# New durations in the engine model that orders a TensorE-bound two-layer kernel

## Chip, cores and metric

One core of one Trainium2 chip. The metric is the device time of one execution in microseconds (us).

## The reference, cut to what matters

One step of a streaming encoder with two layers, for a prompt of 2048 tokens and for 8 samples of 16 new tokens each. The width is 1024, with 8 heads of 128. All arrays are float32.

```python
def trunk(x, c, pos, ...):                       # for the prompt, and again for the samples
    for i in range(2):
        shift, scale, gate = split(silu(c) @ w_ada[i] + b_ada[i])
        h = rmsnorm(x, norm_pre[i]) * (1 + scale) + shift
        if i == 0:    # gated DeltaNet, chunked: conv of q, k, v; then per head
            qkv, z, a, b = split(h @ w_in_gdn)
            q, k, v = silu(causal_conv(qkv)), q and k normalized
            # (I + A)^-1, A strictly lower triangular, applied to v and k; then a scan over the chunks:
            #   u = u_i - w_i @ s;   o = qg_i @ s + qk_i @ u;   s = s * g_i + kd_i^T @ u
            out = (rmsnorm(o) * silu(z)) @ w_out_gdn
        else:         # differential attention, block-causal
            q, k, v, z = split(h @ w_in_diff); q, k = rope(q), rope(k)
            a = softmax(q1 @ k1^T / 8) - lam * softmax(q2 @ k2^T / 8)
            out = (rmsnorm(a @ v) * silu(z)) @ w_out_diff
        x = x + gate * rmsnorm(out, norm_post[i])
```

It returns both outputs and all states, convolution rows, keys and values.

## The kernel before

**Tiles and stages.** The 17 tiles of 128 rows (16 of the prompt, one of the samples) are worked in two halves, of 9 and 8 tiles. Each half passes through four stages: DeltaNet heads (`gdn_heads`), output projection (`out_proj`), attention heads (`diff_heads`), output projection. In the profile these are 100 to 840, 840 to 1000, 1000 to 1640 and 1640 to 1800 us for the first half, and 1800 to 2430, 2430 to 2590, 2590 to 3410 and from 3410 for the second; before 100 us stand the adaptation vectors and the first normalization. Tiles go through the projections in groups of up to three.

**Projections.** `mm3s` (944) makes a float32-like product out of three fp32r matmuls for each 128 rows of the contraction: operands are split into a rounded part and the rest. Weights pass through a staging tile `st` and are split on ACT, VectorE (DVE) and GpSimd (POOL) by `load` (535) into `wq` and `wz`.

**DeltaNet, a head.** `conv` (1182) ends in a Tanh, `gate_out` (1174) is a Silu for z, `decay` (1281) an Exp. `keys` (1242) works out row factors by small GpSimd instructions and powers (tile `sm`). `inverse` (1384) inverts I + A: the 16x16 blocks on VectorE in `blocks` (1335; tiles `Lx`, `Lw`, `Lt`, `Lr`), then merged by small matmuls that use the array as 32x32, 64x32 and 64x64 tiles (`X`, `V`, `W`, `Y`, `F`, `Wf`). `scan` (1504) carries the state: a matmul, `y` on VectorE, a matmul, the copy `r` on ACT, a matmul, the new state `S` on VectorE.

**Attention, a head.** `rotate` applies the rotary embedding (tile `r`), `scores` and `expo` make score pieces of up to 512 keys: VectorE takes the negated maximum `negm`, ACT the exponential `p` with its sum. `weigh` works out the factors `fj`, GpSimd scales the first map's piece, `join` adds the second map's on VectorE, `flip` transposes on TensorE and copies to `at` on ACT or VectorE, `values` multiplies with `vpc`, and `finish` normalizes with a power on GpSimd (`fo`).

**What sets the order.** The order of instructions on TensorE, VectorE, ACT and GpSimd is fixed when the kernel is built, by the class `Weave`. Each of the functions above is a generator, a stream. It yields the engine that it needs next, an event or a tile to wait for. `run` (281) goes in steps: for each stream that can go on it takes the time at which its next instruction could start, the later of the stream's own time and `free_at` of the engine, and lets the earliest one emit its instructions; of equal ones that with the higher priority. Projections have a low priority, so they fill TensorE where nothing else is ready. After every instruction `account` (130) adds its price, `c`, in ns, to the engine's time and notes when its output is ready; `HOP` adds a constant for a result that passes from one engine to another. `either` (206), `copy` (211), `modulate` (699) and `flip` also ask `free_at` which of two engines would be free earlier. The engines then run their instructions in that order on the chip, each waiting for semaphores where an operand is late.

**A duplicate.** A second copy of `queries` (1797) to `scan_sample` of the DeltaNet stage, and of `conv_outputs`, `diff_loads` and the start of `diff_heads`, stands inside a first `diff_heads` (1662). The complete definition of `diff_heads` at line 2149 takes the place of that one before anything is called.

All instructions are emitted through line 105, so the profile gives them that line, and they are told apart by tiles.

Of the kernel before, what the change touches and what calls it, by code (L numbers as in the profile page):

```python
# [12 lines left out]
F32 = mybir.dt.float32  # L13
# [74 lines left out]
class Weave:  # L88
# [23 lines left out]
    def __init__(self, tc, kept):  # L112
        nc = tc.nc
        self.tc = tc
        self.kept = kept
        self.ordered = True
        self.queue_at = self.dma_at = 0.0
        self.parts = {}
        self.free_at = dict(pe=0.0, v=0.0, s=0.0, g=0.0, sy=0.0)
        self.ready = {}  # L120
        self.ev = {}
        self.places = {}
        self.held = {}
        self.streams = []
        self.cur = None
        self.n = 0
        for key, real in (("pe", nc.tensor), ("v", nc.vector), ("s", nc.scalar), ("g", nc.gpsimd), ("sy", nc.sync)):
            setattr(self, key, Weave._Engine(self, key, real))

    def account(self, key, op, args, kw):  # L130
# [4 lines left out]
        n = 1  # L135
# [4 lines left out]
        if key == "pe":  # L140
            if op == "transpose":
                c = (2 if rest[0].dtype == F32 else 1) * max(n, out.shape[0]) * 0.417 + 2
            elif rest[0].dtype == F32:
                c = 4 * max(n, rest[0].shape[-1]) * 0.417 / (4 if out.shape[0] <= 32 else 1)
            else:
                c = max(n, 2 * rest[0].shape[-1]) * 0.417 + 2
        elif key == "v":
            fast = op in ("tensor_copy", "tensor_scalar", "memset") and all(a.space != PSUM for a in rest)
            c = 75 + n * (0.52 if fast else 1.04)
            if op in ("scalar_tensor_tensor", "tensor_scalar") and any(a.shape[-1] == 1 for a in rest):  # L150
                c += 60
            if op == "memset":
                c = 60 + 0.26 * n
        elif key == "s":
# [3 lines left out]
            elif rest[0].space != PSUM:  # L158
                c += 32
        elif key == "g":  # L160
# [12 lines left out]
        start = self.free_at[key]  # L173
# [157 lines left out]
def body(ctx, tc, I, O):  # L331
# [1330 lines left out]
    def diff_heads(hi_, tiles_of, pool, ahead):  # L1662
# [134 lines left out]
        def queries(h, gi, d):  # L1797
            nt = len(tiles_of[gi])
            yield ("conv", h, gi, 0),
            yield ("sq", h, gi),  # L1800
            sq, sm = d["sq"], d["sm"]
            pt = yield from turn(d["q"], nt * P)
            yield from squares(pt, nt * P, sq[:, 1])
            W.free(pt)
            yield "g"
            g.tensor_scalar(sm[:, 3, 0:nt], sq[:, 1, 0:nt], 128.0 * EPS, 512.0 * EPS * EPS, op0=ALU.mult, op1=ALU.add)
            yield ("xq", h, gi),
            W.free(sq)
            for i in range(nt):
                yield from product(d, i, d["q"], d["E"])  # L1810
            W.done(("qk", h, gi))

        def product(d, i, src, out):
            c = slice(i * P, (i + 1) * P)
            ps = yield from bank()
            pe.matmul(ps[:, 0:P], d["k"][:, c], src[:, c], start=True, stop=True)
            yield "v"
            v.scalar_tensor_tensor(out=out[:, i, :], in0=ps[:, 0:P], scalar=d["sm"][:, 2, i:i + 1],
                                   in1=d["E"][:, i, :], op0=ALU.mult, op1=ALU.mult)
            W.free(ps)  # L1820

        def blocks(area, nl):

            X, Wl = (pool.tile([24, 16, 16], F32, name=k, bufs=1) for k in ("Lx", "Lw"))
            wf = Wl.rearrange("p i j -> p (i j)")

            yield "sy"
            sy.dma_start(X[0:nl], bass.AP(area[0].tensor, area[0].offset, [[16 * P + 16, nl], [P, 16], [1, 16]]))
            g.memset(wf[0:nl], 0.0)
            g.memset(wf[0:nl, ::17], 1.0)  # L1830
            yield "v"
            T, R = (pool.tile([24, k], F32, name=nm, bufs=1) for k, nm in ((512, "Lt"), (64, "Lr")))

            def at(a, o, *dims):
                return bass.AP(a.tensor, a.offset + o, [a[0:nl].ap[0], *([st, k] for st, k in dims)])

            def four(a, r, c, nr, ncol):

                return at(a, r * 16 + c, (4 * 17, 4), (16, nr), (1, ncol))

            v.tensor_copy(four(Wl, 0, 3, 3, 1), four(X, 0, 3, 3, 1))
            for j in (2, 1):
                sh = [nl, 4, j, 4 - j]
                t = at(R, 0, (j * (4 - j), 4), (4 - j, j), (1, 4 - j))
                v.tensor_tensor(out=t, in0=four(X, 0, j, j, 1).broadcast_to(sh),
                                in1=four(Wl, j, j, 1, 4 - j).broadcast_to(sh), op=ALU.mult)
                o = four(Wl, 0, j, j, 4 - j)
                v.tensor_tensor(out=o, in0=o, in1=t, op=ALU.add)
            for m in (4, 8):
                def corner(a, s_, r, c):  # L1850
                    return at(a, s_ * 2 * m * 17 + r * m * 16 + c * m, (16, m), (1, m))

                def product(A, B, out):
                    for i in range(8 // m):
                        v.tensor_tensor(out=at(T, i * m ** 3, (m * m, m), (m, m), (1, m)),
                                        in0=A[i][:, :, None, :].broadcast_to([nl, m, m, m]),
                                        in1=B[i].rearrange("p k c -> p c k")[:, None].broadcast_to([nl, m, m, m]),
                                        op=ALU.mult)
                    for i in range(8 // m):
                        v.tensor_reduce(out=out[i], in_=at(T, i * m ** 3, (m * m, m), (m, m), (1, m)), axis=AX.X,  # L1860
                                        op=ALU.add)

                Rs = [at(R, i * m * m, (m, m), (1, m)) for i in range(8 // m)]
                X12, W11, W12, W22 = ([corner(a, i, *rc) for i in range(8 // m)]
                                      for a, rc in ((X, (0, 1)), (Wl, (0, 0)), (Wl, (0, 1)), (Wl, (1, 1))))
                product(X12, W22, Rs)
                product(W11, Rs, W12)
            yield "sy"
            sy.dma_start(bass.AP(area[1].tensor, area[1].offset, [[256, nl], [1, 256]]), wf[0:nl])

        def inverse(h, gi, d):

            nt = len(tiles_of[gi])
            h0, h1 = slice(0, 64), slice(64, P)
            X = yield from new([P, 3, P], "X", NX, "v")
            yield ("E", h, gi),
            for i in range(nt):
                yield from product(d, i, d["k"], X)
            W.done(("xq", h, gi))
            area = yield from W.hold(areas, "area", "sy")  # L1880
            sy.dma_start(area[0][0:nt, 0:P * P].rearrange("t (p c) -> p t c", c=P), X[:, 0:nt])
            yield from blocks(area, 8 * nt)
            W16 = yield from new([P, 3, 16], "W16", 2, "sy")
            sy.dma_start(W16[:, 0:nt], area[1][0:nt].rearrange("t (p c) -> p t c", c=16))
            W.free(area)
            Wt = yield from new([P, 3, 32], "W", 2, "v")
            v.tensor_tensor(out=Wt[:, 0:nt].rearrange("p t (a c) -> p t a c", c=16),
                            in0=W16[:, 0:nt, None, :].broadcast_to([P, nt, 2, 16]),
                            in1=C("same").rearrange("p (a c) -> p a c", c=16)[:, None].broadcast_to([P, nt, 2, 16]),
                            op=ALU.mult)  # L1890
            W.free(W16)
            V = yield from new([P, 3, 32], "V", 2, "v")
            Y = yield from new([P, 3, 32], "Y", 2, "s")
            F = yield from new([P, 3, 64], "F", 2, "s")
            pi = yield from bank("v")

            def area_of(o, n):
                return pi[:, o:o + nt * n].rearrange("p (t c) -> p t c", c=n)

            pa, pb, pf, pt = area_of(0, 32), area_of(96, 32), area_of(192, 64), area_of(0, 64)  # L1900
            quarters = [slice(32 * b, 32 * b + 32) for b in range(4)]

            def each(out, a, b):

                for o, x, y in zip(out, a, b):
                    pe.matmul(o, x, y, start=True, stop=True)

            def parts(t, rows, cols=slice(0, 32)):
                cols = cols if isinstance(cols, list) else [cols] * len(rows)
                return [t[r, i, c] for r, c in zip(rows, cols) for i in range(nt)]  # L1910


            yield "v"
            v.transpose(V.rearrange("p t c -> p (t c)")[:, 0:32 * nt], Wt.rearrange("p t c -> p (t c)")[:, 0:32 * nt])
# [778 lines left out]
```

## Time and profile before

| | us |
|---|---|
| median of 3 runs | 3558.8 |
| lowest, highest | 3554.32, 3575.8 |
| the profiled execution | 3559.35 |
| its span, first to last instruction | 3557.6 |
| mean granted TensorE clock in it | 0.977 |

PE is TensorE's matmuls and PEld its weight loads, DVE is VectorE, POOL is GpSimd. A name such as `ps<-S,q` says which tile is written and which are read, by the program's names. [...]

### The profile page before, as it was taken

To read this page: it belongs to the slowest core of one execution; us is meant where nothing else is said; L and a number is where in the kernel's file an instruction comes from. 1 tells how busy PE (TensorE), PEld (TensorE's weight loads), DVE (VectorE), ACT (ScalarE), POOL (GpSimd) and SP (SyncE) were. 2 spreads that over 40 slices of the span, in tenths; PEclk is the share of its full clock that TensorE was granted. 3 is DMA by queue.
4 is the path that set the end of the run, shared out by engine and by line. 5 is a ranking of instruction groups with operands and counts; after the bars stand their busy time and mean duration, and the time that the engine had idled before them with its cause. 6 is when DMAs were issued, how large, how long until landed. Compare 5 with 4: busy or idle time off the path is not lost.

```text
span 3557.6 us, 79075 instructions
## 1 busy us (share of the span) xinstructions
PE 3390.2 (95%) x28952; PEld 3151.5 (89%) x28952; DVE 2531.9 (71%) x6462; ACT 1763.0 (50%) x5376; POOL 1560.0 (44%) x2836
## 2 busy tenths in 40 slices
PE   5999999999999999999999999998899999999988
PEld 2887789889999999998989899888898999999988
DVE  4677788776576666666567777775588878888872
ACT  3454455553354444444445555553365555555541
POOL 4344444443444344333434554544444444444432
PEclk6999999999999999999999999998999999999999
DMA  5225432236343333444432222224311112111113
GB/s 191 59 64 169 122 77 69 61 98 195 124 130 112 112 114 114 122 120 136 159 91 50 58 62 74 60 75 161 125 42 49 37 55 57 52 52 41 47 57 125
DMA packets 479420, 330.59 MB, mean 93 GB/s; under 512 B 65799, under 2 KB 442143, under 8 KB 479030
## 3 DMA queue, kind: packets, MB, share of 16 engines
q1 hardware_dynamic: 474358, 316.76, 30.0%
q0 software_dynamic: 4672, 8.78, 1.0%
q8 instruction: 227, 3.72, 0.4%
q14 instruction: 163, 1.34, 0.1%
HBM read 233.65 MB, written 91.77 MB: 91 GB/s over the span
## 4 chain that ended last, share of the span: by engine, by line
PE 37%; DVE 7%; POOL 3%; ACT 2%; issue 2%; DMA 1%; SPq 0%; POOLq 0%; DVEq 0%; ACTq 0%
PE ps L105 37%; DVE p L105 1%; DVE negm L105 1%; DVE Lt L105 1%; POOL sm L105 1%; POOL p L105 1%; POOL fo L105 1%; ACT jkg L105 0%; DVE wq L105 0%; DVE rz L105 0%; DVE Lr L105 0%; DMA st<-in_w_in_diff_dram 0%; ACT L105 0%; DMA ro<-og 0%; ACT at L105 0%
## 5 line engine op out<-in xcount | busy, mean ns | idle before, releaser
L105 PE MATMUL ps<-wq,hT 128*128 128x256 f32 x6120 | 851.4, 287 | 4.2 <-DVE r L105 3.1
L105 PEld LDWEIGHTS ps<-wq,hT 128*128 128x128 f32 x6120 | 775.2, 191 | 16.9 <-DVE r L105 3.5
L105 PE MATMUL ps<-hT,wq 128*128 128x384 f32 (+1 forms) x3456 | 696.4, 341 | 2.7 <-ACT ub L105 2.2
L105 PE MATMUL ps<-wz,hT 128*128 128x256 f32 x4488 | 647.4, 292 | 13.3 <-DVE r L105 12.1
L105 PEld LDWEIGHTS ps<-wz,hT 128*128 128x128 f32 x4488 | 581.9, 194 | 23.6 <-DVE r L105 12.8
L105 PEld LDWEIGHTS ps<-hT,wq 128*128 128x128 f32 x3456 | 557.2, 190 | 15.8 <-ACT ub L105 3.1
L105 ACT ACTIVATE p<-ps,negm 128x512 f32<-128x512 f32 (+3 forms) x640 | 397.1, 624 | 225.5 <-DVE negm L105 220.3
L105 DVE TENSOR_REDUCE negm<-ps 128x1 f32<-128x512 f32 (+3 forms) x640 | 375.0, 606 | 66.6 <-PE ps L105 55.5
L105 PE MATMUL ps<-kst,qst 128*128 128x512 f32 (+3 forms) x1280 | 346.7, 379 | 2.8 <-ACT p L105 2.7
L105 POOL TENSOR_SCALAR p<-p,fj 128x512 f32<-128x512 f32 (+2 forms) x320 | 230.8, 732 | 231.4 <-DVE fj L105 165.5
L105 PE MATMUL ps<-vpc,at 128*128 128x128 f32 x2176 | 294.9, 278 | 7.9 <-ACT at L105 6.2
L105 PEld LDWEIGHTS ps<-vpc,at 128*128 128x128 f32 x2176 | 274.5, 193 | 20.7 <-ACT at L105 10.8
L105 DVE SCALAR_TENSOR_TENSOR p<-p,fj,p 128x512 f32<-128x512 f32 (+2 forms) x320 | 248.4, 803 | 23.3 <-POOL p L105 22.8
L105 ACT COPY at<-ps 128x512 f32<-128x512 f32 (+3 forms) x258 | 132.7, 515 | 234.2 <-PE ps L105 228.9
L105 PEld LDWEIGHTS ps<-kst,qst 128*128 128x128 f32 x1280 | 205.8, 190 | 20.2 <-ACT p L105 6.0
L105 POOL TENSOR_TENSOR wq<-st,wq 128x512 fp32r<-128x512 f32 x110 | 150.5, 1370 | 162.0 <-ACT wq L105 92.0
L105 PE MATMUL ps<-cst_ident,p 128*128 128x128 f32 x1224 | 195.3, 277 | 18.9 <-DVE hT L105 7.9
L105 POOL TENSOR_TENSOR fo<-fo,cpow 128x1 f32<-128x1 f32 x280 | 175.5, 627 | 23.3
L105 ACT ACTIVATE jk<-ps 128x128 f32<-128x128 f32 (+1 forms) x212 | 80.4, 379 | 201.6 <-PE ps L105 145.6
L105 PEld LDWEIGHTS ps<-cst_ident,p 128*128 128x128 f32 x1224 | 144.7, 142 | 27.7 <-DVE hT L105 9.1
L105 POOL TENSOR_SCALAR fo<-so 128x1 f32<-128x1 f32 x144 | 32.3, 224 | 269.0 <-ACT jk L105 255.7
L105 POOL TENSOR_SCALAR fo<-so,sm 128x1 f32<-128x1 f32 x136 | 50.3, 370 | 211.5 <-ACT jkg L105 211.2
(328 smaller groups left out, 6413.2 us busy)
## 6 DMA issues: line engine op xcount, KB each, us to landing
st<-in_w_in_gdn_dram SPq DMA_DIRECT2D x128, 256.0 KB
st<-in_w_in_diff_dram SPq DMA_DIRECT2D x256, 128.0 KB
x<-x SPq DMA_DIRECT2D x34, 512.0 KB
wz<-in_w_ada_dram SPq DMA_DIRECT2D x16, 1024.0 KB
sp<-in_cache_k_dram SPq DMA_DIRECT2D x64, 256.0 KB
sp<-in_cache_v_dram SPq DMA_DIRECT2D x64, 256.0 KB
zg<-zt SPq DMA_DIRECT2D x68, 128.0 KB
og<-o SPq DMA_DIRECT2D x136, 64.0 KB
```

Source lines behind the costliest of these rows:

```text
L105: r = f(*args, **kw)
```

## The change

Prices in `account` get new values, and a change of the array's tiling on TensorE and a change of function table on ACT get a price of their own, `hold`, that is added before the instruction's start. Two fields are added, for the tiling and the table in use. The duplicate described above (498 lines) is taken out. Nothing else is changed.

```diff
@@ Weave.__init__
         self.parts = {}
+        self.tiling = P, P
+        self.table = None
@@ Weave.account
-        n = 1
+        n, hold = 1, 0
...
         if key == "pe":
+            rows, cols = (next(k for k in (32, 64, P) if a <= k) for a in (rest[0].shape[0], rest[0].shape[-1]))
             if op == "transpose":
-                c = (2 if rest[0].dtype == F32 else 1) * max(n, out.shape[0]) * 0.417 + 2
+                c = max(n, out.shape[0]) * (0.85 if rest[0].dtype == F32 else 0.65)
             elif rest[0].dtype == F32:
-                c = 4 * max(n, rest[0].shape[-1]) * 0.417 / (4 if out.shape[0] <= 32 else 1)
+                c = 4 * max(n, rest[0].shape[-1]) * 0.434 / (4 if cols == 32 else 1) / (2 if rows == 32 else 1)
             else:
-                c = max(n, 2 * rest[0].shape[-1]) * 0.417 + 2
+                c = max(n, 192) * 0.434 + 6
+
+            if (rows, cols) != self.tiling:
+                hold = 100 if self.tiling == (P, P) else 120
+                self.tiling = rows, cols
         elif key == "v":
             fast = op in ("tensor_copy", "tensor_scalar", "memset") and all(a.space != PSUM for a in rest)
             c = 75 + n * (0.52 if fast else 1.04)
             if op in ("scalar_tensor_tensor", "tensor_scalar") and any(a.shape[-1] == 1 for a in rest):
                 c += 60
+            if op == "tensor_tensor" and len(out.shape) == 4 and out.shape[-1] <= 8:
+                c = 75 + 2.06 * n
...
         elif key == "s":
             c = 60 + 0.83 * n + (95 if "accum_out" in kw else 0)
             if any(isinstance(kw.get(k), bass.AP) for k in ("bias", "scale")):
                 c += 85
             elif rest[0].space != PSUM:
                 c += 32
+
+            table = {AF.Silu: "silu", AF.Exp: "exp", AF.Ln: "ln", AF.Tanh: "silu exp"}.get(kw.get("func"))
+            if table and self.table not in table.split():
+                hold = 1280
+                self.table = table.split()[-1]
         elif key == "g":
...
             else:
-                c = (240 if len(rest) > 1 else 155) + 0.84 * n
+                c = (240 if len(rest) > 1 or n < 8 else 155) + 0.84 * n
             if op == "tensor_tensor" and kw.get("op") == ALU.pow:
-                c = 300 + 160 * n
+                c = 390 + 170 * n
...
-        start = self.free_at[key]
+        start = self.free_at[key] + hold
@@ inside the first diff_heads
-        def queries(h, gi, d):
...
```

## Rows read from the trace of the kernel before

**Rows 1.** The page: busy us, share and instructions of each engine.
```profile
PE 3390.2 (95%) x28952; PEld 3151.5 (89%) x28952; DVE 2531.9 (71%) x6462; ACT 1763.0 (50%) x5376; POOL 1560.0 (44%) x2836
```
**Rows 2.** Busy time by stage; columns as in the first line.
```profile
core 0: us, PE busy (x) PEld busy (x) DVE busy (x) ACT busy (x) POOL busy (x), PEclk, DMA share, GB/s
0.00:100.00 100.00, 60.14 (x343) 33.19 (x343) 45.84 (x105) 36.08 (x79) 40.20 (x64) 0.71 0.56 179
100.00:840.00 740.00, 716.33 (x6462) 641.54 (x6461) 569.69 (x1592) 381.15 (x1243) 326.17 (x720) 0.99 0.33 93
...
1000.00:1640.00 640.00, 639.26 (x5796) 612.02 (x5795) 439.57 (x1238) 298.83 (x954) 261.90 (x491) 1.00 0.41 117
...
1800.00:2430.00 630.00, 599.46 (x5601) 551.28 (x5600) 477.40 (x1306) 346.81 (x1130) 306.33 (x627) 0.97 0.25 66
...
2590.00:3410.00 820.00, 793.90 (x6076) 748.50 (x6074) 675.91 (x1592) 465.88 (x1383) 377.92 (x582) 1.00 0.18 50
```
**Rows 3.** TensorE's waits, 100 to 840: us in total, times, longest us.
```profile
PE ps L105 <- DVE y L105: 5.1, 3, 2.8
...
PE ps L105 <- ACT r L105: 2.7, 6, 0.6
PE ps L105 <- DVE V L105: 2.5, 5, 0.8
PE ps L105 <- ACT ub L105: 1.9, 1, 1.9
PE ps L105 <- ACT Y L105: 1.6, 2, 1.4
...
PE ps L105 <- ACT zt L105: 1.1, 2, 0.6
```
**Rows 4.** TensorE's waits, 1800 to 2430.
```profile
PE ps L105 <- DVE S L105: 9.5, 4, 5.7
PE ps L105 <- DVE y L105: 6.1, 7, 2.8
PE ps L105 <- DVE V L105: 5.9, 2, 4.5
PE ps L105 <- ACT r L105: 3.7, 8, 0.9
```
**Rows 5.** TensorE's waits, 2590 to 3410.
```profile
PE ps L105 <- ACT at L105: 5.4, 8, 0.8
...
PE ps L105 <- POOL fo L105: 0.8, 1, 0.8
```
**Rows 6.** Busy time, 900 to 950, columns as in rows 2.
```profile
900.00:950.00 50.00, 50.00 (x422) 50.00 (x421) 23.50 (x47) 18.91 (x47) 20.32 (x29) 1.00 0.30 102
```
**Rows 7.** The weight loads' waits, whole span: us in total, times, longest us.
```profile
PEld ps L105 <- issue: 72.8, 222, 4.8
```
**Rows 8.** Instruction groups on VectorE: busy us, mean ns of one, idle before.
```profile
L105 DVE TENSOR_TENSOR Lt<-Lw,Lr 24x512 f32<-24x512 f32 x40 | 48.8, 1220 | 1.4
...
L105 DVE TENSOR_TENSOR Lt<-Lw,Lr 24x64 f32<-24x64 f32 x80 | 21.5, 305 | 0.0
```
**Rows 9.** Timeline of one block inverse: start us, us, instruction, idle before.
```profile
1850.98 2.57 POOL L105 TENSOR_TENSOR wq<-st,wq 128x512 fp32r<-128x512 f32 x2 [0.99 <-ACT wq L105]
...
1851.17 2.50 DVE L105 TENSOR_TENSOR Lt<-Lw,Lr 24x64 f32<-24x64 f32 x2
...
1853.96 1.00 DVE L105 TENSOR_TENSOR Lt<-Lx,Lw 24x512 f32<-24x512 f32 x1
...
1856.79 0.67 DVE L105 TENSOR_REDUCE Lw<-Lt 24x64 f32<-24x512 f32 x1
...
1858.14 0.93 PE L105 MATMUL ps<-V,X 32*32 32x32 f32 x24 [4.49 <-DVE V L105]
```
**Rows 10.** Instruction groups on ACT, columns as in rows 8.
```profile
L105 ACT ACT_TABLE_LOAD x64 | 82.1, 1283 | 8.2 <-DMA c<-in_c_sample_dram 3.7 <-DVE q L105 3.5
```
**Rows 11.** Timeline of ACT around one table load, columns as in rows 9.
```profile
1866.44 0.20 ACT L105 ACTIVATION_READ_ACCUMULATOR jkg<-ps 128x1 f32 x1
1866.66 1.28 ACT L105 ACT_TABLE_LOAD   x1
1867.95 0.42 ACT L105 ACTIVATE E<-E 128x256 f32<-128x256 f32 x1
```
**Rows 12.** Instruction groups on GpSimd, columns as in rows 8.
```profile
L105 POOL TENSOR_TENSOR fo<-fo,cpow 128x1 f32<-128x1 f32 x280 | 175.5, 627 | 23.3
```
**Rows 13.** Busy time around the wait for S, columns as in rows 2.
```profile
2406.00:2412.00 6.00, 0.53 (x2) 0.53 (x3) 5.79 (x17) 0.21 (x1) 0.61 (x2) 0.50 0.42 134
2412.00:2430.00 18.00, 18.00 (x187) 15.78 (x186) 5.68 (x17) 6.27 (x26) 6.88 (x11) 0.80 0.29 87
```
**Rows 14.** The page: the group of the softmax joins, all widths.
```profile
L105 DVE SCALAR_TENSOR_TENSOR p<-p,fj,p 128x512 f32<-128x512 f32 (+2 forms) x320 | 248.4, 803 | 23.3 <-POOL p L105 22.8
```

More of the change, by code (lines that the diff above doesn't have):

```diff
@@ L1795, in rotate @@
             W.done(("k", h, t))
-        def queries(h, gi, d):
[L1798 to L1914, printed above, removed]
-            yield "pe"
-            each(parts(pa, quarters), parts(X, quarters, quarters), parts(V, quarters))
-            yield "s"
-            s.copy(Y[:, 0:nt], pa)
-            yield "pe"
-            each(parts(pb, quarters), parts(Y, quarters), parts(Wt, quarters))
-            yield "v"
-            v.copy_predicated(Wt[:, 0:nt], C("lev").bitcast(U32)[:, None, :].broadcast_to([P, nt, 32]), pb)
-            v.transpose(V.rearrange("p t c -> p (t c)")[:, 0:32 * nt], Wt.rearrange("p t c -> p (t c)")[:, 0:32 * nt])
-            upper, lower = quarters[0::2], quarters[1::2]
-            yield "pe"
-            each(parts(pa, lower), parts(X, upper, lower), parts(V, upper))
-            Wf = d["Wf"] = yield from new([P, 3, P], "Wf", NWF, "g")
-            e = W.either(nt * P)
-            yield e
-            getattr(W, e).tensor_tensor(
-                out=Wf[:, 0:nt].rearrange("p t (a c) -> p t a c", c=32),
-                in0=Wt[:, 0:nt, None, :].broadcast_to([P, nt, 4, 32]),
-                in1=C("quart").rearrange("p (a c) -> p a c", c=32)[:, None].broadcast_to([P, nt, 4, 32]), op=ALU.mult)
-            yield "s"
-            for r in lower:
-                s.copy(Y[r, 0:nt], pa[r])
-            yield "pe"
-            each(parts(pb, upper), parts(Y, lower), parts(Wt, lower))
-            yield "s"
-            for r, c in zip(upper, lower):
-                s.copy(Wf[r, 0:nt, c], pb[r])
-            for i in range(nt):
-                yield "pe"
-                pe.transpose(pf[h0, i], Wf[h0, i, h0], ident[0:64, 0:64])
-            yield "s"
-            s.copy(F[h0, 0:nt], pf[h0])
-            yield "pe"
-            for c in range(64, P, 32):
-                each(parts(pt, [slice(c, c + 32)], slice(0, 64)), parts(X, [h0], slice(c, c + 32)), parts(F, [h0], h0))
-            W.free(X)
-            yield "s"
-            s.copy(F[h1, 0:nt], pt[h1])
-            yield "pe"
-            each(parts(pf, [h0], h0), parts(F, [h1], h0), parts(Wf, [h1], h1))
-            yield "s"
-            s.copy(Wf[h0, 0:nt, h1], pf[h0])
-            W.free(Wt, V, Y, F, pi)
-            W.done(("inv", h, gi))
@@ L1962, in used @@
-        def used(h, gi, i):
-            d = U[h, gi]
-            d["left"] -= 1
-            if d["left"] == 0:
-                W.free(d["k"], d["q"], d["nv"], d["kd"], d["E"], d["Wf"])
-        def scans():
-            for h in range(H):
-                state = None
-                if hi_ > 0:
-                    state = pool.tile([P, P], F32, name="S", bufs=3)
-                    sy.dma_start(state, st_d[h])
-                for gi, tiles in enumerate(tiles_of):
-                    for ev in ("kd", "nv", "qk", "inv"):
-                        yield (ev, h, gi),
-                    d = U[h, gi]
-                    d["norm"] = len(tiles)
-                    for i, t in enumerate(tiles):
-                        if t == S_T:
-                            W.spawn(scan_sample(h, gi, i, d), 4)
-                        else:
-                            ns = pool.tile([P, P], F32, name="S", bufs=3)
-                            yield from scan(h, gi, i, d, state, ns)
-                            state = ns
-                if last:
-                    sy.dma_start(O["state_gdn_prompt"][0, 0, h], state)
-                else:
-                    sy.dma_start(st_d[h], state)
```

273 lines of the change are left out of this document (removed).

## Prediction

> **What bounds the kernel now.** I read the busy times first: TensorE is busy for 3390.2 of 3557.6 us and VectorE, next, for 71% [rows 1]. The time goes down only where TensorE idles or runs at half clock, so the table by stage comes next [rows 2]. The start (0 to 100 us) idles for 40 us and has a granted clock of 0.71. The first DeltaNet stage (100 to 840) idles for 740.00 - 716.33 = 23.7 us, the second (1800 to 2430) for 30.5 us at a clock of 0.97. The first attention stage (1000 to 1640) idles for 0.7 us, the second (2590 to 3410) for 26.1 us. Third, what TensorE waited for in those stages, because each wait tells which result the order of instructions put too early. In the DeltaNet stages these are mostly VectorE results on the path of the state and of the block inverse (y, V, S: 5.1 + 2.5, then 9.5 + 6.1 + 5.9 us) and ACT results (2.7 + 1.9 + 1.6 + 1.1, then 3.7 us) [rows 3, 4]. In the second attention stage they are short, such as eight of at most 0.8 us for the transposed weights `at`, 5.4 us in all [rows 5].
>
> The change touches no computation. The removed 498 lines are a second copy of functions, inside an earlier `diff_heads` that the later definition of that name replaces; no instruction comes from them: nothing. Everything else is prices inside `account`, and prices act in two ways: which stream `run` lets emit next on an engine, and which engine `either`, `copy`, `modulate` and `flip` choose. So nearly all instructions stay the same in number and kind, and what can change is waiting, plus a little work moved between VectorE, ACT and GpSimd.
>
> **TensorE's prices.** In a stretch of little but 256-column matmuls there are 422 starts in 50.00 us, 118.5 ns each [rows 6]. Old price 256 x 0.417 + 2 = 109 ns, new 256 x 0.434 + 6 = 117 ns. No matmul becomes faster by this. A change of array tiling now costs 100 to 120 ns of model time. In the trace the weight loads sit idle 222 times for "issue" alone, 72.8 us in all, 0.33 us each [rows 7]. `run` ranks streams by when they could start, without this extra, so it doesn't group the small matmuls: I leave these 73 us where they are. If the new order had fewer or more switches, I'd bound that by a quarter of them either way, 18 us.
>
> **The block inverse on VectorE.** `blocks` emits its VectorE instructions in one piece, 40 times for three tiles and 8 times for two. Its largest instruction (24x512) was priced 75 + 1.04 x 512 = 607 ns and takes 1220 on average [rows 8]; new price 75 + 2.06 x 512 = 1130. With its two reductions at 607 both before and after, the m = 8 part goes from 2430 to 3474 ns. In the one block that I follow it takes from 1853.96 to 1857.46, 3.5 us, so that part is now priced right. The same block shows the consequence: the 32x32 matmuls on V idle 4.49 us for it [rows 9]. But it also shows what no price holds: a pair of 24x64 products, 305 ns each on average [rows 8], took 2.50 us while GpSimd ran two weight subtractions (2.57 us). So I count half of the VectorE waits as repaired: y, S and V together are 5.1 + 2.5 + 9.5 + 6.1 + 5.9 = 29.1 us [rows 3, 4], half is 14.5 us. Bounds: 0 (all of it is the stretching) and 29.1; a loss by the new order as such is counted once, with the sum.
> [...]
>
> **ACT's table loads.** There are 64, 1283 ns each, priced 0 before and 1280 now [rows 10]. Between silu and exp they alternate in both DeltaNet stages, and as `run` doesn't rank by this extra either, I expect 50 to 80 of them. What goes is the surprise. ACT's waits by TensorE there sum to 2.7 + 1.9 + 1.6 + 1.1 + 3.7 = 11.0 us [rows 3, 4]; the 6.4 us for `r` are 14 short waits for a copy whose price is unchanged, so about 4.6 us can be loads and the instructions queued behind them, and ACT's delay reaches TensorE through VectorE too. I take 6 us, bounds 0 and 11.
> [...]
>
> **GpSimd's prices.** The power goes from 460 to 560 ns (627 measured, [rows 12]), small instructions by 85 ns. GpSimd is busy 44% [rows 1] and in the longest stage TensorE waits for its powers 0.8 us in all [rows 5]; over four such stages worth 0 to 3 us, I take 0.
>
> **The clock.** [...] Over the second DeltaNet stage 0.97 means 0.03 x 630 = 19 us, over the first 0.01 x 740 = 7 us [rows 2], of which idle time is a part that costs nothing. If half of the waits go, I take a third of these 26 us: 9 us, bounds 0 and 20.
>
> **Sum.** 14.5 + 6 + 9 = 29.5 us, all on the path because TensorE sets the end. Start, attention and the output stages: their order is drawn anew too; I take 0 on balance, bounds 15 us either way. The profiled execution took 3559.35 us, 0.6 above the median of the three runs, so both give the same: 3559.4 - 29.5 = **3530 us**, 0.8% less.
>
> **Rivals.** *The gaps close fully:* all 29.1 + 11.0 us of these waits, 20 us of clock, and a good half (14 us) of the second attention stage's 26.1: 74 us, 3485. For it: prices and trace agree closely for m = 8 and the loads. Against: the stretching, and that most prices (the softmax ones among them) stay as they were. *The gain is hidden:* the waits have moved elsewhere, 0 to 12 us, about 3553. For it: 2.50 us for a pair of 0.6. *Slower, by the lost cushion in the softmax chain:* until now a result priced X was covered by X/109 filler matmuls of 118.5 real ns, 8.7% more time than X; now by X/117, 1.3% more. One softmax piece of 512 keys is priced 607 (maximum) + 665 (exp) + 670 (GpSimd scale) + 667 (join) + 485 (copy) = 3094 ns, unchanged, so its cover shrinks by 7.4%, 0.23 us. There are 320 pieces [rows 14], 74 us if every one lands on TensorE: with the 29.5 gained, 3604. It decides from 128 pieces on (29.5 / 0.23). For it: the second attention stage already has such waits [rows 5]. Against: the first idles 0.7 us in 640, so there is more cover than this cushion, and a late result costs only what is not covered by the rounding to whole groups of three matmuls.
>
> **How the numbers follow.** The forecast (3512 to 3548) 0.47, full closing (below 3512) 0.25, hidden (3548 to 3572) 0.15, slower (above 3572, centred on 3604) 0.13. About 1% (36 us: below 3523, above 3594) is what a measurement of this kernel can tell from no change. A third of the forecast's chance lies below 3523, with the full closing 0.40; above 3594 only the softmax rival, with 0.09 of its 0.13; the rest, 0.51, within. Range 3470 (full closing, with 15 us from start and attention) to 3594.
>
> **What would show it.** Right: the table by stage has 10 to 20 us less idle in the DeltaNet stages, the waits for y, S and V halve, the clock of 1800 to 2430 rises to 0.98 or 0.99, matmul groups keep their counts, and table loads stay between 50 and 80. Wrong: the waits for S and V stay as long with GpSimd products beside them (hidden), or the first attention stage, now idle 0.7 us, idles 20 us or more behind `at`, `p` and `negm` (slower). The forecast falls as a whole if the number of tiling switches or table loads changes by more than a third, or if work moved between VectorE and GpSimd decides.

## The result, and the profile after

The changed kernel takes 3591.94 us (median of 5 runs, 3591.56 to 3597.81) where the kernel before, beside it, took 3565.01 (5 runs, 3554.32 to 3575.8): ratio 1.0083, interval 1.0068 to 1.0098. It is 0.8% slower, and the forecast was 0.8% faster. The profiled executions stand 3590.1 to 3557.6 us by their spans, 32.5 us apart.

The page of the changed kernel has the same 28952 matmuls as [rows 1]. They are busy 22.3 us longer (what matmuls take longer at half clock is part of that, and is split off below), and the rest of the 32.5 us is idle time:

```profile
PE 3412.5 (95%) x28952; PEld 3164.6 (88%) x28952; DVE 2555.1 (71%) x6473; ACT 1761.6 (49%) x5373; POOL 1558.1 (43%) x2820
```

To compare stage by stage, the stretches have to begin and end at the same piece of work. I cut both kernels at the first convolution of a half, the first rotation, the first convolution of the second half, its first rotation, and the end of the last output rows (each stretch is one stage with its output projection). Busy time in these stretches, before:

```profile
core 0: us, PE busy (x) PEld busy (x) DVE busy (x) ACT busy (x) POOL busy (x), PEclk, DMA share, GB/s
94.00:965.00 871.00, 840.75 (x7500) 763.24 (x7498) 637.62 (x1711) 427.34 (x1353) 381.23 (x792) 0.99 0.35 102
965.00:1792.00 827.00, 817.30 (x7229) 784.14 (x7230) 548.09 (x1463) 382.23 (x1162) 341.65 (x613) 0.99 0.42 126
1792.00:2557.00 765.00, 723.28 (x6610) 670.43 (x6608) 545.49 (x1427) 393.98 (x1249) 362.95 (x706) 0.97 0.28 80
2557.00:3551.00 994.00, 954.73 (x7332) 904.36 (x7332) 754.69 (x1759) 524.30 (x1537) 432.83 (x666) 0.99 0.19 57
```

And after:

```profile
95.00:1013.00 918.00, 860.04 (x7498) 773.93 (x7496) 634.27 (x1702) 425.12 (x1356) 383.00 (x790) 0.95 0.33 97
1013.00:1853.00 840.00, 822.58 (x7235) 784.73 (x7236) 560.05 (x1461) 385.38 (x1163) 348.98 (x615) 0.99 0.42 124
1853.00:2602.00 749.00, 721.44 (x6604) 671.08 (x6602) 553.69 (x1443) 394.31 (x1247) 353.54 (x692) 0.98 0.29 82
2602.00:3584.00 982.00, 950.67 (x7332) 902.05 (x7332) 759.78 (x1767) 521.28 (x1533) 434.38 (x665) 1.00 0.20 58
```

The first number behind the stretch is its length. The first DeltaNet stage got 47 us longer, the first attention stage 13; the second DeltaNet stage got 16 us shorter, the second attention stage 12. Length less PE busy is idle time: in the first stage it goes from 30.3 to 58.0 us, and its granted clock from 0.99 to 0.95. The trace's record of the clock has two levels, 1 and 0.5 (18 stretches at 0.5 before, 21 after); a granted clock between them is a mean over the stretch, and half clock is the level 0.5. The record splits the loss further: I count half of the time that TensorE works at half clock as lost. That is my estimate; for the 149 matmuls at the end of this document it gives 0.48 x 25 = 12 us where 24.76 - 14.48 = 10.3 were measured. By that count, with the cuts at the exact instants instead of whole us, the first stage lost 27.8 us to more idle time and 20.6 us to more half clock; the second DeltaNet stage won 13.7 us of idle time and lost 1.2 to the clock; the second attention stage won 8.9 and 4.6. What is left when idle time and half clock are taken off differs by under 5 us in each stage, so next to nothing is dearer work. The second half of the tiles gained 28 us, about as much as was forecast in all, though only 16 of them in a stage where the forecast put its gain; the first half lost 60.

**The waits.** TensorE's waits in the first DeltaNet stage after (101 to 851, a stretch that like that of [rows 3] ends with the last steps of the scan):

```profile
PE ps L105 <- ACT r L105: 13.2, 3, 10.1
PE ps L105 <- DMA wz<-in_w_ada_dram: 12.0, 5, 3.4
PE ps L105 <- DVE y L105: 4.2, 2, 2.9
PE ps L105 <- DVE adaC L105: 3.1, 1, 3.1
...
PE ps L105 <- DVE V L105: 1.5, 2, 0.9
PE ps L105 <- DVE S L105: 1.5, 2, 1.1
```

The same scan steps lie in both stretches, but not the same amount of filling work:

```profile
101.00:851.00 750.00, 705.11 (x6225) 623.56 (x6226) 557.63 (x1572) 367.84 (x1222) 317.77 (x709) 0.95 0.30 85
```

These are 6225 matmuls where [rows 2] has 6462. The scan ended some 11 us later than before, and 237 matmuls, most of them of projections, were left to run behind it; that is where the rest of the 47 us shows.

In the second (1861 to 2467, answering to [rows 4]):

```profile
PE ps L105 <- DVE y L105: 7.6, 10, 3.2
PE ps L105 <- ACT zt L105: 1.4, 1, 1.4
...
PE ps L105 <- ACT r L105: 1.3, 4, 0.4
PE ps L105 <- ACT ub L105: 1.3, 1, 1.3
PE ps L105 <- DVE V L105: 1.1, 4, 0.4
PE ps L105 <- ACT Y L105: 1.1, 2, 0.7
...
PE ps L105 <- DVE S L105: 0.6, 2, 0.4
```

And in the second attention stage (2635 to 3442, answering to [rows 5]), where the waits for `at` shrink, those for `p` grow and new ones for `kst` come in:

```profile
PE ps L105 <- DVE p L105: 6.1, 11, 1.2
PE ps L105 <- DVE kst L105: 4.4, 5, 1.8
...
PE ps L105 <- ACT at L105: 1.1, 3, 0.7
```

The views of [rows 5] and of [rows 3] have, before, for `p` and for the weights of the adaptation vectors (`in_w_ada`):

```profile
PE ps L105 <- DVE p L105: 4.0, 7, 0.8
```

```profile
PE ps L105 <- DMA wz<-in_w_ada_dram: 4.6, 3, 3.9
```

In the second DeltaNet stage y, S and V fall from 21.5 to 9.3 us. The waits for ACT there don't fall: `r` goes from 3.7 to 1.3 us, but `r`, `zt`, `ub` and `Y` together from 4.6 to 5.1. In the first stage y, S and V stay (7.6 to 7.2), and two kinds of wait are new in size: one for `r`, and those for the adaptation vectors (their weights and `adaC`). They make 21 of the 28 us of added idle time.

The longest, 10.1 us for `r`, can be read from ACT's timeline (start, us, instruction, in brackets its idle time and what ended it):

```profile
776.95 0.62 ACT L105 CAST wz<-st 128x512 fp32r<-128x512 f32 x1 [0.25 <-DMA st<-in_w_in_gdn_dram]
780.80 0.62 ACT L105 CAST wq<-st 128x512 fp32r<-128x512 f32 x1 [3.23 <-DMA st<-in_w_out_gdn_dram]
782.72 0.62 ACT L105 CAST wz<-st 128x512 fp32r<-128x512 f32 x1 [1.30 <-DMA st<-in_w_in_gdn_dram]
...
787.56 0.53 ACT L105 ACTIVATE ub<-k 128x384 f32<-128x384 f32 x1 [1.50 <-DVE k L105]
787.99 0.25 ACT L105 COPY r<-ps 128x128 f32<-128x128 f32 x1
```

Ahead of the copy `r`, whose operand TensorE had finished at about 778, the model had put casts of weights whose transfers were still under way: ACT's queue stood for 3.23 + 1.30 us for two transfers and 1.50 for `k`, and the scan's next matmul with it. The change gives transfers no new price. The same place in busy time, with what follows:

```profile
777.80:788.30 10.50, 0.39 (x3) 0.10 (x2) 8.49 (x16) 3.52 (x10) 5.96 (x7) 0.50 0.43 117
788.30:800.00 11.70, 11.01 (x118) 9.73 (x119) 8.28 (x20) 4.76 (x20) 3.68 (x5) 0.68 0.19 57
800.00:810.00 10.00, 10.00 (x97) 8.43 (x96) 4.63 (x14) 7.57 (x21) 5.92 (x16) 1.00 0.21 59
```

At 0.68 over 11.70 us the stretch behind the wait costs, by the same estimate, another 0.32 x 11.70 = 3.7 us.

The groups that the prediction counted on hold: weight loads idle for "issue" 74.9 us, 223 times ([rows 7]: 72.8, 222), the 24x512 product takes 1204 ns on average ([rows 8]: 1220), and there are 56 table loads ([rows 10]: 64):

```profile
L105 ACT ACT_TABLE_LOAD x56 | 71.8, 1283 | 8.2 <-DMA c<-in_c_sample_dram 3.5 <-DVE q L105 3.0 <-DVE k L105 0.6
```

### The profile page after: what moved, and what is told of

Its sections match the earlier page's. It is cut to its first block, busy times and chain, and to the rows that moved or that the text cites. A ratio compares the mean times of both kernels' runs of the same rounds, so it can differ in the third digit from the quotient of the medians.

```text
span 3590.1 us, 79032 instructions
## 1 busy us (share of the span) xinstructions
PE 3412.5 (95%) x28952; PEld 3164.6 (88%) x28952; DVE 2555.1 (71%) x6473; ACT 1761.6 (49%) x5373; POOL 1558.1 (43%) x2820
## 4 chain that ended last, share of the span: by engine, by line
PE 36%; DVE 8%; DMA 2%; POOL 2%; issue 2%; ACT 1%; SPq 0%; POOLq 0%; DVEq 0%; ACTq 0%
PE ps L105 36%; DVE p L105 2%; DVE negm L105 1%; DVE Lt L105 1%; POOL p L105 1%; POOL fo L105 0%; DVE wq L105 0%; ACT p L105 0%; DMA ro<-zg 0%; DMA ro<-og 0%; DVE rz L105 0%; DVE Lw L105 0%; DVE kst L105 0%; DVE r L105 0%; SPq L105 0%
## 5 line engine op out<-in xcount | busy, mean ns | idle before, releaser
L105 PE MATMUL ps<-wz,hT 128*128 128x256 f32 x4488 | 639.2, 290 | 10.9 <-DVE r L105 9.6
L105 PEld LDWEIGHTS ps<-hT,wq 128*128 128x128 f32 x3456 | 564.5, 191 | 15.6 <-issue 2.1
L105 POOL TENSOR_SCALAR p<-p,fj 128x512 f32<-128x512 f32 (+2 forms) x320 | 240.8, 764 | 287.1 <-DVE fj L105 232.4
L105 POOL TENSOR_TENSOR wq<-st,wq 128x512 fp32r<-128x512 f32 x104 | 142.6, 1372 | 148.9 <-ACT wq L105 81.9
L105 POOL TENSOR_SCALAR fo<-so,sm 128x1 f32<-128x1 f32 x136 | 59.3, 436 | 245.7 <-ACT jkg L105 244.0
```

What stands on the lines that cost most here:

```text
L105: r = f(*args, **kw)
```

## The experiments

Times are medians; the ratio is to the kernel before, run beside it. "First half" and "second half" are the parts of the profiled span up to and after the last output row of the first half of the tiles.

| kernel | prices: first half, second half | us | ratio, interval | first half | second half |
|---|---|---|---|---|---|
| before | old, old | 3561.8 to 3566.4 | | 1791 | 1767 |
| VectorE +1 ns | old, old | 3569.62 | 1.0010 (0.9997 to 1.0024) | 1813 | 1753 |
| VectorE -1 ns | old, old | 3584.23 | 1.0045 (1.0031 to 1.0060) | 1818 | 1766 |
| after | new, new | 3591.94 | 1.0083 (1.0068 to 1.0098) | 1853 | 1737 |
| after, ACT +1 ns | new, new | 3586.75 | 1.0057 (1.0040 to 1.0074) | 1839 | 1751 |
| after, ACT -1 ns | new, new | 3567.33 | 1.0005 (0.9992 to 1.0017) | 1815 | 1750 |
| new half, old half | new, old | 3624.41 | 1.0169 (1.0149 to 1.0189) | 1856 | 1764 |
| old half, new half | old, new | **3538.78** | 0.9934 (0.9913 to 0.9954) | 1793 | 1746 |
| old DeltaNet 1, then new | mixed, new | 3547.42 | 0.9951 (0.9936 to 0.9967) | 1806 | 1735 |
| matmul prices alone | part, part | 3610.46 | 1.0132 (1.0115 to 1.0148) | 1839 | 1770 |
| tiling price alone | part, part | 3599.99 | 1.0104 (1.0085 to 1.0123) | 1825 | 1776 |
| table loads alone | part, part | 3579.83 | 1.0039 (1.0016 to 1.0063) | 1819 | 1764 |
| VectorE's price alone | part, part | 3643.35 | 1.0225 (1.0206 to 1.0244) | 1849 | 1801 |

**One group of prices at a time.** Each kernel is the one before with one part of the change as it stands in the diff above. GpSimd's prices alone were not tried.

Matmul prices:

> Only the new TensorE durations (matmuls, transposes) on the kernel before; no price for a change of tiling, all other prices old. Theory A (the loss is made in the first DeltaNet stage, because the adaptation weights are taken up later and the z projections, which fill TensorE, are used up behind them): if it is the matmul durations that delay them, this kernel shows most of the loss, +20 to +35 us, the first out projection starts 30 us or more later than before, and the last adaptation matmul lies after 500 us instead of 442. Theory B (the cushion: matmuls priced truer cover the softmax chain less): +20 us or more, but lost in the two attention stages, with the first DeltaNet stage unchanged within 10 us. Theory C (the order is drawn anew by any change of prices, and where the time lands is chance): anywhere from -25 to +35, with places that change from kernel to kernel.

Tiling:

> Only the price for a change of the array tiling (100 or 120 ns) on the kernel before. Theory A: if it is this price that makes the model's TensorE look full in the first DeltaNet stage, +20 to +35 us here and the adaptation matmuls later than before; else within 10 us of before. Theory B: no loss, since no matmul duration changes: within 10 us. Theory C: anywhere from -25 to +35.

Table loads:

> Only the price of ACT's table loads (1280 ns) on the kernel before. The prediction's step gave this part alone 6 us of gain (0 to 11), with a part of the clock's 9: -5 to -10 us, ACT waits of TensorE in the DeltaNet stages shorter, 50 to 80 loads. Theory A: no loss here. Theory C: anywhere from -25 to +35.

The block inverse's products:

> Only the price of the four-dimensional VectorE products of the block inverse (75 + 2.06 n) on the kernel before. The prediction's step gave this part alone 14.5 us of gain (0 to 29), with a part of the clock's 9: -10 to -20 us, and half of the 29.1 us of waits for y, S and V gone. Theory A: no loss, the adaptation matmuls end before 460 us. Theory C: anywhere from -25 to +35, and the waits for y, S and V are no shorter than before or have moved to others.

Measured by the medians (before, beside them, 3566.41): +44, +34, +13 and +77 us. All four are slower, and together (+27) they are less so than three of them alone: the parts don't add up, so a term for each edit can't be right. The two from which the prediction took its gain lost. With the VectorE price alone TensorE waits longer, not less, in the second DeltaNet stage for y, V and S together (1850 to 2560; 26.4 us against 21.5 before), and longer for `r`:

```profile
PE ps L105 <- DVE y L105: 17.1, 7, 7.6
PE ps L105 <- ACT r L105: 7.7, 9, 3.8
PE ps L105 <- DVE V L105: 6.3, 5, 2.0
...
PE ps L105 <- DVE S L105: 3.0, 2, 2.8
```

Theory A's place is right in all four (the first DeltaNet stage with its output projection is 24 to 61 us longer than before) but its cause is not: with the VectorE price, the largest loss, the last adaptation matmul comes at 423, earlier than the 442 of before, and with the tiling price at 685, the latest of all, with a smaller loss. Theory B falls for the matmul prices: 35 of their loss lie in the first DeltaNet stage, 11 in the first attention stage with its projection, 7 in the second.

**Prices that say nothing.** Is it the values, or that the order was drawn anew? One nanosecond on every instruction of an engine tells nothing about the engine.

```diff
-            c = 75 + n * (0.52 if fast else 1.04)
+            c = 76 + n * (0.52 if fast else 1.04)
```

> The kernel before with every VectorE price 1 ns higher (76 instead of 75 ns plus the elements), which says nothing new about the engines. Theory C (the order is drawn anew by any change, and the order of before is a draw better than most): slower than before, by +10 to +70 us as the four parts alone were (+13 to +77), with the loss in the DeltaNet stages. Theory D (the new values themselves do harm, each a little): within 10 us of before, since nothing is said about the engines.

And 74, the other way:

> The kernel before with every VectorE price 1 ns lower (74). Theory C: slower than before by +10 to +70 us, by another amount than the kernel with 76, and lost at other places. Theory D: within 10 us of before.

The same on the changed kernel, on ACT (60 to 61, and to 59):

> The changed kernel with every ACT price 1 ns higher (61 instead of 60 ns plus the elements). Theory C: 15 us or more away from the changed kernel, on either side, and still slower than before. Theory D: within 10 us of the changed kernel. If the new prices are better in themselves (the prediction's terms, 29.5 us) and only the draw hid it, the redrawn versions of after lie some 30 us below the redrawn versions of before on average.

> The changed kernel with every ACT price 1 ns lower (59). As for the kernel with 61: theory C 15 us or more away from the changed kernel on either side, theory D within 10 us of it.

The ns alone moves the kernel before by +4 and +18 us, the changed one by -5 and -25. Two of the four lie within theory D's 10 us, but as sums of larger moves: +22 in the first half and -13 in the second, -14 and +13. So D falls, and C's mechanism holds with a smaller size than I gave it. The +77, +44 and +34 of the parts lie outside of what these redraws did, so some harm of the values themselves is likely there; each is one draw. Three orders with old prices have a mean of 3573 us (with 3566 for before), three with new ones 3582: of the 26 us between the two kernels some 9 are the prices by this count, the rest is that before is the best of its three and after the worst. The three of a kind lie 18 and 25 us apart, so 9 can't be told from 0. None of the six kernels so far that change prices of before for the whole run (two redraws, four parts) is faster than it: before seems to be a well-drawn order, against which most redraws look like a loss. In the first half the redraws of before lost 22 and 27 us without any new duration.

**Halves exchanged.** `account` of before and of after stand side by side, and a flag chooses one; it changes where the second half begins, so up to there the order is exactly that of the one kernel.

```diff
+    def account(self, key, op, args, kw):
+        (self.account_new if self.new else self.account_old)(key, op, args, kw)
...
     def layers(hi_, groups):
+        W.new = hi_ == 1
```

> Old prices for the first half of the tiles, new prices from the start of the second half on, so the order of the first half is that of before to the instruction. Over the kernels so far the first half (up to the last row of its second output projection) took 1791, 1813 and 1818 us with old prices (before and its two redraws) and 1853, 1839 and 1815 with the new ones; the second half 1767, 1753 and 1766 with old, 1737, 1750 and 1750 with new. Theory E (the new prices are of use in the second half and do harm in the first): the first half stays at 1791, the second takes 1737 to 1750: 15 to 30 us faster than before. Theory C alone (only the luck of the draw): the second half falls anywhere from 1737 to 1800, so from 30 us faster to 35 slower, 0 in the middle.

With `hi_ == 0`:

> New prices for the first half of the tiles, old ones from the start of the second half on. The first half has the order of the changed kernel to the instruction and so its time, 1853 us against 1791 of before (+62). Theory E: the second half takes 1753 to 1767 us as with old prices, in all +50 to +62 against before, slower than the changed kernel by 15 to 30 us. Theory C alone: second half 1737 to 1800.

Both came out about as theory E says: 3538.78 us, 23 us faster than before and 53 faster than after, and 3624.41, 63 us slower than before. They don't exclude theory C, in whose range both second halves lie. The first joins the better half of either kernel, and beats both. Its stretches, cut as above:

```profile
93.00:968.00 875.00, 845.22 (x7499) 766.74 (x7498) 635.47 (x1710) 428.42 (x1353) 381.10 (x792) 0.98 0.35 102
968.00:1794.00 826.00, 816.36 (x7231) 783.71 (x7232) 548.64 (x1464) 383.02 (x1163) 343.23 (x613) 0.99 0.43 127
1794.00:2549.00 755.00, 724.28 (x6608) 673.82 (x6606) 553.22 (x1444) 389.33 (x1241) 356.71 (x696) 0.97 0.29 81
2549.00:3532.00 983.00, 952.91 (x7332) 903.62 (x7332) 759.45 (x1766) 520.97 (x1533) 433.99 (x663) 0.99 0.20 58
```

Against chance speaks the second half over all orders drawn: it took 1735 to 1757 us in the eight kernels that have the new prices whole there (those of the table and the three below) and 1753 to 1767 in the four different orders with old ones, means 1745 and 1762. The ranges overlap a little, so a single order can come out either way, but on average the new prices are worth some 17 us there.

**What a wait costs.** Copies of the same block on ACT, unknown to the model, go ahead of `r` in `scan`, so the order of everything else stays.

```diff
+            if hi_ == 0 and (h, gi, i) == (4, 1, 1):
+                for _ in range(40):
+                    tc.keep_in_program_order(nc.scalar.copy(r_, pc[:, P:2 * P]))
             s.copy(r_, pc[:, P:2 * P])
```

A first pair, with the same expectations, had this edit in the second copy of `scan`, which nothing calls: two repeats of before, at 1.0009 (0.9995 to 1.0024) and 1.0014 (1.0001 to 1.0027), spans 3558.7 and 3563.1. So the same order repeats within 0.14% and some 6 us of span. Then, in the function that runs:

> The kernel before in its own order, with 40 more copies of the same 128x128 block on ACT (262 ns each, 10.5 us in all) ahead of one result r in the DeltaNet scan of the fifth head, in the function that runs. Theory F (a wait of TensorE costs itself and then a stretch at half clock behind it): +13 to +15 us, a stretch at half clock begins there and 3 to 5 us of the loss lie in it. If waits cost only themselves: +10.

Ratio 1.0031 (1.0017 to 1.0045): 3580.61 against 3565.71, +14.9 us. TensorE's timeline at the place:

```profile
575.64 0.80 PE L105 MATMUL ps<-r,kd 128*128 128x128 f32 x2 [11.52 <-ACT r L105]
```

And four stretches about it:

```profile
560.00:564.00 4.00, 4.00 (x26) 3.80 (x24) 3.93 (x10) 2.04 (x6) 1.43 (x3) 1.00 0.03 6
564.00:575.00 11.00, 0.13 (x1) 0.00 (x0) 1.47 (x5) 9.85 (x37) 0.58 (x2) 0.63 0.02 2
575.00:600.00 25.00, 24.36 (x205) 22.36 (x206) 15.37 (x46) 10.90 (x37) 9.19 (x21) 0.89 0.33 80
600.00:616.00 16.00, 16.00 (x167) 15.25 (x165) 14.22 (x36) 9.78 (x30) 7.49 (x16) 1.00 0.40 106
```

The wait is 11.5 us, the clock falls within it (0.63 over those 11 us, 1.00 in the 4 before), and by the same estimate 0.11 x 25 = 2.8 us are lost behind it: 14.3, as expected. The interval of the ratio (6 to 16 us) would allow 11.5 as well; the 2.8 comes from the trace's 0.89. With ten short ones:

> The kernel before in its own order, with 6 more such copies (1.6 us) ahead of ten results r, spread over the eight heads of the first DeltaNet stage, 15.7 us in all; TensorE's own work covers a part of each. Theory F with any wait enough: each is followed by a stretch at half clock and the loss is 1.5 to 3 times the waits that the trace shows. Theory F with only long or crowded waits enough: the loss equals the added waits, 8 to 16 us, and the granted clock of the stage stays at 0.99.

Ratio 1.0020 (1.0008 to 1.0032), +8.1 us. The first stage of this kernel, its waits for `r` (2.7 us in [rows 3]) and its clock:

```profile
PE ps L105 <- ACT r L105: 14.3, 16, 1.6
```

```profile
95.00:965.00 870.00, 836.65 (x7491) 757.75 (x7491) 633.62 (x1706) 441.96 (x1410) 378.97 (x790) 0.99 0.35 101
```

11.6 us of added waits cost 8.1 us (3 to 11 by the interval) and no clock (0.99 as before): no more than themselves, partly because other waits shrank (y from 5.1 to 3.3 us). So the reading with "only long or crowded waits enough" holds here, for waits of up to 1.6 us.

**The adaptation work raised.** It tests what was left of theory A: that late adaptation weights, and the z projections behind them, make the first half slow.

```diff
                 if x[1] == "ada":
+                    W.cur["prio"] = -6
                     yield from ada_apply(x, *x[2:], bank)
+                    W.cur["prio"] = 1
                     continue
```

> The changed kernel (all new prices) with one edit: while it works on adaptation vectors, the stream that also does the z projections gets a high priority instead of the lowest, so these matmuls come as soon as their weights are there and the z projections follow earlier. Theory A (the first half is slow under the new prices because TensorE waits for adaptation weights and the fillers come late): the waits for these weights and for adaC, 15.1 us in the changed kernel, go below 5, the last adaptation matmul comes before 460 us instead of 537, and the first half falls from 1853 to 1815 or less (30 us or more gained). Theory C (draw): the first half lies anywhere between 1805 and 1860, also with those waits gone, because others take their place.

Measured 3553.42 us, 0.9965 (0.9952 to 0.9979): 38.5 us faster than after and 0.35% faster than before. The first half takes 1814 us, the waits for these weights 4.4 us, and the last such matmul comes at 391. On the redraw with ACT +1 ns:

> The changed kernel with every ACT price 1 ns higher (a redraw that took 3586.75 us, first half 1839) and the adaptation work raised as before. Theory A (late adaptation weights and fillers make the first half slow under the new prices): the first half comes to 1820 or less again, as it did from 1853 to 1813 without the extra ns, and the whole to 3545 to 3570. Theory C (the gain of 38 us was a lucky draw): the first half stays between 1820 and 1860.

3575.5 us, 1.0035 (1.0022 to 1.0049). The first half came from 1839 to 1811, as theory A says; the whole is over its 3570, since the second half took 1757. The first stage of that redraw without the edit, and with it:

```profile
94.00:1000.00 906.00, 865.19 (x7499) 782.01 (x7498) 633.20 (x1700) 414.93 (x1347) 386.26 (x793) 0.96 0.34 98
```

```profile
94.00:974.00 880.00, 841.35 (x7507) 764.07 (x7503) 635.47 (x1693) 433.60 (x1362) 392.82 (x797) 0.99 0.35 101
```

Length less busy is 40.8 and 38.7 us: nearly all of the 26 us between these two executions is clock, 0.96 to 0.99. The medians of the two kernels lie only 11 us apart, so part of it is luck of the execution (see the end). And without the edit this redraw had only 3.8 us of waits for adaptation weights and adaC, so it wasn't those waits that the edit took away. With old prices in the first half:

> Old prices in the first half, new ones in the second, and the adaptation work raised: the candidate to beat all. Theory A, with early fillers useful under the old prices too: first half 1780 to 1791, second 1735 to 1750, 3515 to 3542. Theory C (the first half of before is the best of its draws, and any edit leaves it): first half 1800 to 1820, 3540 to 3570.

3563.48 us, 0.9996 (0.9983 to 1.0009); first half 1816, second 1744. Theory A falls for old prices: the edit costs 25 us there. With the edit the first half takes 1811 to 1816 us under either prices, where without it new ones took 1815 to 1856 and old ones 1791 to 1818. The edit helps the orders that were slow; that late adaptation work is what made them slow isn't shown.

**Old prices in the first DeltaNet stage alone.** The flag is set behind `gdn_heads` and stays.

```diff
             gdn_heads(hi_, groups, pool, out_loads(0, hi_))
...
+            W.new = True
             out_proj(0, hi_, groups, pool, diff_loads(hi_)[:3])
```

> Old prices for the first DeltaNet stage alone, new ones for all that follows (from the first output projection on). The kernel with old prices for the whole first half took 3538.78 us. Theory E' (the new prices do harm in the first DeltaNet stage only): the first output projection starts at 873 us as before, its stage and the first attention stage take as long as before within 5 us, the second half 1737 to 1750: 3530 to 3545. Theory E'' (they do harm in the whole first half, as the changed kernel lost 17 us more between 873 and 1791): 3550 to 3565.

3547.42 us: the first rows of the first output projection are scaled at 872 (873 before) and the second half takes 1735, but the first attention stage with its projection takes 842 us, 16 more than before. So E' falls in that part, and E'' is nearer there. It is no matter of the draw: this part takes 837 to 842 us in all six different orders with the new prices there and 824 to 830 in the four with old ones. The matmul prices alone give 838, the tiling and the table prices alone 834 each, VectorE's alone 826.

## Why the prediction was wrong, point by point

- **The sum, "I take 0 on balance, bounds 15 us either way"**, is the step that failed, with "a loss by the new order as such" inside of it. It was held against the start, attention and output stages only; for the DeltaNet stages the sum counted repairs and no loss. The first DeltaNet stage with its output projection took 47 us longer. One nanosecond on VectorE's prices, which repairs nothing, cost 19 and 25 us in this same stretch. In the attention stages with their projections 13 us lost and 12 won cancel, so 0 was right there by luck.
- **The time**, 3591.94, lies just inside the stated range (to 3594), by luck too: above 3572 only the softmax rival had a chance, and its place was wrong.
- **The block inverse** (-14.5): half of y, S and V was right for the second stage, 21.5 to 9.3 us, and wrong for the first, 7.6 to 7.2. By itself the price lost 77 us, so the gain isn't the price's alone. The lower bound, all of these waits due to the stretching beside GpSimd (2.50 us for the pair in [rows 9]), would have left them as they were; in the second stage they fell by 12.2 us.
- **ACT's table loads** (-6): `r`, `Y`, `ub` and `zt` were 11.0 us; `r` alone fell from 3.7 to 1.3 in the second stage, where the other three took up what it won, and rose from 2.7 to 13.2 in the first, behind casts that wait for transfers. Alone the price lost 13 us, about as a redraw does.
- **The clock** (-9): wrong in sign: +20.6 us in the first stage, +18 over all four. No run shows the third of 26 us that the term takes; it was my estimate. One place before has a wait and half clock together, 0.50 in the wait for S and 0.80 over the 18 us behind [rows 13]; in the changed kernel the clock cost 1.2 us more in the second DeltaNet stage too, where idle time fell by 13.7 us. I let the clock follow the repaired waits and not the waits that a new order brings.
- **GpSimd** (0) and **the tilings** (0): issue waits 72.8 to 74.9 us, as said; the tiling price still moves the order, +34 us alone.
- **The removed copy** (nothing): an edit inside that copy ran as before, within 0.14%.
- **"Slower, by the lost cushion"** came near in time (3604) but not by its place: the second attention stage got faster, and in the first no wait for `at`, `p` or `negm` carries the 13 us. That the first attention stage loses under truer matmul prices, and that these alone give 838 there, is the part of it that stands. What fills those 13 us is open: waits make some 8 of them.

Right was that nothing changes in kind: equal matmuls, 56 loads, waits and clock alone moved. The second DeltaNet stage has the signs that the prediction named: y, S and V halved, 13.7 us less idle, a clock of 0.98 for 0.97. That the prices rather than the draw gave them is likely from the means of the second halves, and not shown for this stage by itself.

Open: why the same prices help the second half and not the first. Of the first stage's 47 us the draws can explain most (the stretch takes 880 to 918 us in the three draws with new prices, 871 to 896 in those with old), but which of its waits the new prices make and which the draw isn't shown. Also not tried: after without the VectorE price, and redraws of each part.

## What to carry to other kernels

Where a greedy model sets the order, a better price is first of all a new draw: change a price by a nanosecond a few times on both sides, and only then read what a duration is worth. Compare by stage, cut at the same work, and take each stage's order from the prices that serve it; here that beat both kernels. In the first DeltaNet stage ten short waits (11.6 us, each at most 1.6) cost 8.1 us, no more than themselves, and one long one (11.5 us) came with half clock, some 2.8 us behind it by estimate, so I would count a long wait with the half clock behind it.

## What the runs showed of the hardware

I hadn't expected that orders with nearly the same idle time (40.8 and 38.7 us above) differ by so much clock (0.96 and 0.99). Nor this, in the execution with the one added wait, some 120 us ahead of that wait, where TensorE is busy for 24.76 of 25 us:

```profile
430.00:440.00 10.00, 7.66 (x70) 6.23 (x68) 6.36 (x16) 5.51 (x23) 7.37 (x17) 1.00 0.30 79
440.00:465.00 25.00, 24.76 (x149) 18.81 (x150) 12.40 (x41) 8.74 (x31) 7.29 (x21) 0.52 0.18 47
```

In the kernel before the same 149 matmuls ran at full clock, in 14.5 us:

```profile
439.90:454.39 14.49, 14.48 (x149) 11.34 (x150) 11.28 (x35) 8.63 (x31) 6.79 (x19) 1.00 0.22 57
```

In the profiled execution of the exchanged halves, whose order is that of before up to there, the clock fell at the same place:

```profile
435.00:460.00 25.00, 25.00 (x153) 19.26 (x153) 12.52 (x44) 8.85 (x32) 7.28 (x21) 0.52 0.18 47
```

Of six such executions (before, the two repeats, the exchanged halves, old prices in the first DeltaNet stage, the one added wait) three fell here (0.52, 0.52 and 0.80 over 25 us) and three ran at 1.00. So the clock's falls differ from one execution to the next for the same instructions, and this one alone costs some 10.5 us (25.00 against 14.49); it is part of why that execution's span (3580.9) is 23 us longer than that of before, while the medians differ by 15. Half-clock counts of single executions, those above too, carry that much luck.
